# Toeplitz blocks sent through DRAM, and half of the first layer's gate projection in plain float32, in an S5 / HGRN2 / attention trunk

## Chip, cores and metric

The kernel runs on one core of one Trainium2 chip. The metric is the device time of one execution in microseconds (us), as the median of several runs. A core has these engines: PE (TensorE, with PEld for its weight loads), DVE (VectorE), ACT (ScalarE), POOL (GpSimd) and SP (SyncE, which here only issues DMAs).

## What is computed

Four layers on a sequence of 512 tokens of width 1024, each h = h + RMSNorm(branch(RMSNorm(h))). The mixers are S5 (layers 0 and 3), HGRN2 (layer 1) and sliding-window attention (layer 2). The change is in the S5 branch, cut here to what matters:

```python
proj = h @ w_in                      # 1024 -> 2048
u, z = proj[..., :1024], proj[..., 1024:]
xr, xi = B(u)                        # per group of 16 channels: 64 complex states
sr, si = scan(a, xr, xi)             # s_t = a * s_(t-1) + x_t, complex, along the sequence
y = C_re(sr) - C_im(si) + d_skip * u
y = gelu(y)
y = y * sigmoid(y @ w_glu + b_glu)   # the gate projection, 1024 -> 1024
return (y * silu(z)) @ w_out
```

All inputs and the output are float32.

## The kernel before, in words

**Activations** lie with channels on partitions, [128, 8, 512]. A projection runs as 128 x 512 outputs (two of 256 columns for the first four) over eight steps k of 128 channels each. Most matmuls are in float32r with both operands split into a high and a low part (hi, lo), three matmuls a step: hi*hi, hi*lo, lo*hi (`ws_steps`, line 233). Weights are split when they have landed (`w_conv`): ACT copies raw into whi (line 183), DVE subtracts it into wlo (line 184). The input projection of layer 0 is the exception (`plain`, line 156): x stays in one float32 tile xf, the raw weights are used as they are, and a step is one float32 matmul, which the trace shows as two records.

**Weights** come in chunks (256 columns, two pieces of 512 KB; `w_load`, line 153, on SP's queue) in the order of a list: for layer 0 eight chunks of s5_in, four of s5_glu, two of s5_out. Rings of buffers hold them: wraw 3, whi 4, wlo 4. In layer 0 the first piece of each s5_in chunk lies in whi, the second in wraw, and wlo holds parameters (prm) and a table (vt) of the S5 blocks.

**The S5 mixer** works on eight blocks b of eight groups. The sequence is cut into 64 chunks of eight steps. For a block, `s5_v` builds on DVE, from parameters that SP loads (prm), the coefficients q (with a second product q2 of POOL) and the table vt. `s5_taps` takes products of it on PE (kps), copies them to kt (ACT), transposes vt to v (tps) and kt to ktp, and adds the skip term (ksb, line 785); then eight DMAs (line 790) write growing parts of ksb into toep, a Toeplitz block whose zeros were set once. `s5_w` builds w on DVE. `s5_rot` makes the rotation factors. `s5_u` takes the projection out of PSUM, writes it to DRAM (ub, line 819) and reads it back in another layout (u, line 823). `s5_core` multiplies (xps), scans on DVE (line 852), forms the states (spre, line 862), and sums two products, u by toep and states by w (yps, lines 875 and 877), to y, with GELU on ACT and transposes for each pair of blocks (ytp, line 892). In layer 3 the tables were computed ahead, and `s5_load` only loads them.

**The order** of PE, DVE, ACT and SP in an S5 layer is written by a planner (`Flow`). Each piece of work is a generator that yields steps: an engine ("P", "V", "A", "D" for SP's DMAs), an assumed duration, and marks it waits for. The planner always takes the step that can start first, at equal times the one with the lower rank. It counts 0.4 us from one engine to another and 4.5 us behind a DMA. The engines then run in that order. The blocks have ranks 0 to 75, the rest of the input projection (`s5_rest`) 100, the first half of the gate projection (`s5_glu_first`, chunks 0 and 1) 110. A weight load is issued where the code of `s5_rest` or `s5_glu_first` stands, without a step of its own.

One wait is written by hand (line 725): in layer 0 `s5_v` of block b + 1 waits for kt of block b, since kt uses the buffer q12b, in which q2 lies (line 764). In layer 3 kt has its own buffer.

```python
yield "V", 1.3, (m["ap"],) + ((m["kt", b - 1],) if b and j == 0 else ())
```

For the gate projection `s5_yparts` splits y into yh (ACT) and yl (DVE). yl lies in the buffer of x ("xh") and yh in that of its low part ("xl"), so yl can be written only when the input projection is done (mark "rest"). Chunks 2 and 3 of the gate and all of the output projection (`out_proj`, line 248) come after the planned part, in an order that the framework chooses.

**The start** (`run`): x comes in four blocks of 128 tokens, the weights of chunks 0 and 1 between the second and the third. `norm_stats` squares each on ACT (line 279), takes the reciprocal root on POOL (`rstd`) and scales it, in layer 0 on ACT (line 284), in the others on DVE (line 286); `norm_xt` transposes it on PE (line 301), and ACT moves it to xf (line 305).

Of the kernel before, what the change touches and what calls it, by code (L numbers as in the profile page):

```python
# [17 lines left out]
P = 128  # L18
T = 512
# [90 lines left out]
class Trunk:  # L110
# [30 lines left out]
    def w_load(self, i):  # L141
# [17 lines left out]

    def w_conv(self, i):  # L160
# [13 lines left out]
        for raw in raws:  # L174
# [5 lines left out]
            else:  # L180
                hi = self.wpool.tile(shape, F32R, tag="whi", name="whi", bufs=4)
                lo = self.wpool.tile(shape, F32R, tag="wlo", name="wlo", bufs=4)
# [80 lines left out]
    def norm_stats(self, L, tbs, h):  # L263
# [17 lines left out]
        for i, tb in enumerate(tbs):  # L281
            if L == 0:

                nc.scalar.activation(out=xs[:, tb, :], in_=h[:, tb, :], func=AF.Copy, scale=r[:, i:i + 1])
            else:
                self.last_xs = nc.vector.tensor_scalar(out=xs[:, tb, :], in0=h[:, tb, :], scalar1=r[:, i:i + 1], scalar2=None, op0=ALU.mult)
# [336 lines left out]
    def s5_load(self, b, m):  # L623

        nc, s = self.nc, self.scr
        yield "D", 0.2, (m["states", b - 2],) if b > 1 else ()
# [8 lines left out]

    def s5_convs(self, i0, m):

        m["cv", 1].t = 0.0
        for c in range(2, 8):
            yield "A", 2.1, (m["cd", c - 2],) if c > 1 else ()  # L640
            yield "V", 2.6, ()
            self.w_conv(i0 + c)
            self.w_load(i0 + c + 1)
            yield m["cv", c]

    def s5_open(self, j):
# [5 lines left out]
        self.kt = None  # L652
        if j == 0:
            self.s5_params(j)
        else:
            self.s5t = {}
            self.kt = 1
# [6 lines left out]
        self.sp, self.tp, self.cp = [], [], []  # L664
        self.md = s.tile([P, 8, 64], F32, tag="mdec", name="mdec", bufs=1)
        nc.gpsimd.memset(self.md[:, :, 0:1], 0.0)
        for i in range(2):
            t = s.tile([P, 8, 8, 16], F32, tag=f"toep{i}", name="toep", bufs=1)
            nc.gpsimd.memset(t, 0.0)
            self.tp.append(t)  # L670
# [7 lines left out]
    def s5_rot(self, pr, m):  # L678
# [23 lines left out]
        for i in range(2):  # L702

            b = 2 * pr + i
            yield "D", 0.3, (m["states", b - 2],) if pr else ()
# [7 lines left out]
    def s5_v(self, j, b, m):  # L713
# [11 lines left out]
        yield "V", 1.3, (m["ap"],) + ((m["kt", b - 1],) if b and j == 0 else ())  # L725
# [26 lines left out]
    def s5_taps(self, b, m):  # L752
# [11 lines left out]
        kt = self.tab.tile([P, 2, 128], F32, tag="q12b" if self.kt is None else "kt", name="kt", bufs=1)  # L764
# [45 lines left out]
    def s5_u(self, b, ps, m):  # L810
# [6 lines left out]
        yield "D", 0.2, ()  # L817
# [3 lines left out]
        yield "D", 0.2, (m["y", b - 3],) if b > 2 else ()  # L821
# [79 lines left out]
    def s5_rest(self, L, ps, m):  # L901
# [5 lines left out]
        def chunk(c):  # L907
            if plain:
                return self.w_next("s5_in")
# [5 lines left out]
        for half in range(2):  # L915
            c = slice(half * 256, half * 256 + 256)
            for b in range(4):
                if half == 0 and b == 2:
                    if not plain:
                        yield "P", 0.0, (m["cv", 1],)  # L920
# [13 lines left out]
        for c in range(6):  # L934
            if not plain:
                yield "P", 0.0, (m["cv", c + 2],)
# [19 lines left out]
    def s5_yparts(self, pr, yh, yl, free, m):  # L956

        nc, y = self.nc, self.y
        for k in (2 * pr, 2 * pr + 1):
# [4 lines left out]
            yield "V", 0.7, (m["rest"],)  # L964
# [5 lines left out]
    def s5_glu_first(self, glu, y, i0, early, m):  # L970

        w = []
        for c in range(2):
            if early and c == 0:
                yield "A", 2.1, (m["cd", 6],)
                yield "V", 2.6, ()
                self.w_conv(i0 + 8)
                self.w_load(i0 + 9)
                continue
            yield "V", 2.6, (m["rest"],)  # L980
            self.w_conv(self.wi + c)
            self.w_load(self.wi + c + 1)
# [6 lines left out]
        for k in range(KB):  # L989
            for fb in range(4):  # L990
                if k < 6:
                    yield "P", 0.68, (m["yk", k],)
                    if k == 0:
                        steps[fb] = self.ws_steps(glu[fb], w[fb // 2], fb % 2, (y[0][0], y[1][0]), 0, T)
                    next(steps[fb])
        for fb in range(4):
            if fb == 2:
                yield "V", 2.6, ()
                self.w_conv(self.wi)
                self.w_load(self.wi + 1)  # L1000
            for k in (6, 7):
                yield "P", 0.68, (m["yk", k],)
                next(steps[fb])

# [656 lines left out]
```

## Time and profile before

| | us |
|---|---|
| three runs, median (lowest to highest) | 1086.48 (1085.96 to 1090.13) |
| the profiled execution | 1089.59 |
| its span in the trace | 1087.8 |
| S5 of layer 0, from the start to the output projection | 239.4 |
| busy: PE, DVE, ACT, POOL | 1027.0, 746.8, 505.2, 104.4 |

The runs are timed without a profile. The rows come from the profiled execution, whose own time is that of its span and what lies around it. All times in a row are in us from the start of the span unless ns is written.

### The profile page before, as it was taken

The numbers are of one execution on the slowest core, as the hardware profiler recorded it, in microseconds if no ns is written. First come the engines' busy times: TensorE is split into PE (matmuls) and PEld (weight loads), VectorE is DVE, ScalarE is ACT, GpSimd is POOL, SyncE is SP. The second block draws the span as 40 slices with busy tenths as digits, with TensorE's granted clock in tenths as the row PEclk, the third lists the DMA queues.
The fourth block names the chain that finished last, engine by engine and source line by source line (L and its number), as shares of the span: only waits on it lengthen the run. The fifth ranks groups of instructions, "written<-read, shape, count | busy, mean of one in ns | idle before, by whom it ended". The sixth has DMA issues, their size and how long they took to land.

```text
span 1087.8 us, 17048 instructions
## 1 busy us (share of the span) xinstructions
PE 1027.0 (94%) x6480; PEld 816.6 (75%) x6480; DVE 746.8 (69%) x1454; ACT 505.2 (46%) x937; POOL 104.4 (10%) x164
## 2 busy tenths in 40 slices
PE   5999995999999999999999999999999989897997
PEld 3855554777998798998978986666678867676875
DVE  6487789584689778888865664556656687754752
ACT  5234345554552314323244433588844556555531
POOL 2000000030200100000011021100002111000300
PEclk9999997999999999999999999999999999998999
DMA  6375333434432323424253354211223777634221
GB/s 236 79 207 147 96 102 96 157 112 150 149 106 64 126 83 107 156 73 144 67 188 141 97 134 115 59 58 45 79 83 132 212 189 197 205 96 161 96 97 58
DMA packets 70577, 133.31 MB, mean 123 GB/s; under 512 B 28896, under 2 KB 40032, under 8 KB 69472
## 3 DMA queue, kind: packets, MB, share of 16 engines
q1 hardware_dynamic: 65664, 119.04, 35.5%
q10 hardware_dynamic: 4832, 13.19, 3.7%
q8 instruction: 51, 0.84, 0.3%
q14 instruction: 30, 0.25, 0.1%
HBM read 100.51 MB, written 20.15 MB: 111 GB/s over the span
## 4 chain that ended last, share of the span: by engine, by line
PE 66%; DVE 14%; ACT 7%; DMA 5%; issue 5%; POOL 2%; SPq 2%; ACTq 1%; DVEq 0%; POOLq 0%
PE pj L233 27%; PE ops L248 14%; PE zps L248 4%; PE vps L248 3%; PE sps L1138 3%; DVE wlo L184 3%; PE scps L1346 3%; ACT whi L183 2%; PE aops L1382 2%; DMA rsw<-rraw 1%; PE yps L877 1%; SPq L790 1%; PE yps L875 1%; PE ptp L1377 1%; DVE sg L1067 1%
## 5 line engine op out<-in xcount | busy, mean ns | idle before, releaser
L233 PE MATMUL pj<-xh,whi 128*128 128x512 f32 (+1 forms) x496 | 179.9, 364 | 1.2 <-ACT xh L305 0.6
L184 DVE TENSOR_TENSOR wlo<-wraw,whi 128x1024 fp32r<-128x1024 f32 x116 | 144.6, 1262 | 52.4 <-ACT whi L183 45.2
L233 PE MATMUL pj<-xl,whi 128*128 128x512 f32 (+1 forms) x496 | 175.1, 354 | 2.1 <-DVE xl L311 2.1
L233 PE MATMUL pj<-xh,wlo 128*128 128x512 f32 (+1 forms) x496 | 175.4, 354 | 0.0
L183 ACT ACTIVATE whi<-wraw 128x1024 fp32r<-128x1024 f32 x116 | 120.7, 1056 | 73.2 <-PE pj L233 33.5
L233 PE MATMUL pj<-xf,wraw 128*128 128x512 f32 (+1 forms) x320 | 119.6, 524 | 0.4 <-ACT xf L305 0.4
L233 PEld LDWEIGHTS pj<-xh,whi 128*128 128x128 f32 x496 | 93.8, 190 | 17.5 <-issue 5.4
L233 PEld LDWEIGHTS pj<-xl,whi 128*128 128x128 f32 x496 | 94.4, 190 | 13.9 <-DVE xl L311 2.9
L233 PEld LDWEIGHTS pj<-xh,wlo 128*128 128x128 f32 x496 | 94.2, 190 | 13.5 <-issue 1.7
L248 PE MATMUL ops<-whi,gh 128*128 128x512 f32 x256 | 101.7, 398 | 2.7 <-ACT gh L1069 2.1
L248 PE MATMUL ops<-wlo,gh 128*128 128x512 f32 x256 | 100.7, 394 | 1.1 <-DVE wlo L184 1.0
L248 PE MATMUL ops<-whi,gl 128*128 128x512 f32 x256 | 100.5, 395 | 0.0
L233 PEld LDWEIGHTS pj<-xf,wraw 128*128 128x128 f32 x320 | 61.0, 198 | 42.1 <-issue 36.7
L248 PEld LDWEIGHTS ops<-whi,gh 128*128 128x128 f32 x256 | 48.2, 188 | 13.9 <-ACT gh L1069 3.0
L248 PEld LDWEIGHTS ops<-wlo,gh 128*128 128x128 f32 x256 | 48.2, 188 | 13.1 <-DVE wlo L184 2.7
L248 PEld LDWEIGHTS ops<-whi,gl 128*128 128x128 f32 x256 | 48.1, 188 | 11.2 <-DVE gl L1070 0.9
L233 PE MATMUL pj<-yh,whi 128*128 128x512 f32 x128 | 51.1, 399 | 0.0
L233 PE MATMUL pj<-yh,wlo 128*128 128x512 f32 x128 | 50.1, 392 | 0.0
L233 PE MATMUL pj<-yl,whi 128*128 128x512 f32 x128 | 50.1, 392 | 0.0
L354 DVE TENSOR_TENSOR yg<-ops,gpost 128x512 f32<-128x512 f32 x32 | 21.8, 687 | 38.8 <-ACT junk L352 38.8
L248 PE MATMUL vps<-wlo,xh 128*128 128x256 f32 x160 | 45.3, 283 | 0.0
L248 PE MATMUL vps<-whi,xl 128*128 128x256 f32 x160 | 45.3, 283 | 0.0
(279 smaller groups left out, 2100.4 us busy)
## 6 DMA issues: line engine op xcount, KB each, us to landing
wraw<-in_s_in SPq DMA_DIRECT2D x32, 512.0 KB, 4.7
wraw<-in_hg_in SPq DMA_DIRECT2D x32, 512.0 KB, 3.6
wraw<-in_at_in SPq DMA_DIRECT2D x20, 512.0 KB, 4.3
wraw<-in_s_glu SPq DMA_DIRECT2D x16, 512.0 KB, 3.8
wraw<-in_s_out SPq DMA_DIRECT2D x16, 512.0 KB, 3.5
hd<-h SPq DMA_DIRECT2D x6, 1024.0 KB, 4.0
prm<-in_s_bc SPq DMA_DIRECT2D x16, 256.0 KB, 3.8
ub<-ut SPq DMA_DIRECT2D x16, 256.0 KB, 3.7
```

Source lines behind the costliest of these rows:

```text
L183: nc.scalar.activation(out=hi, in_=raw, func=AF.Copy)
L184: nc.vector.tensor_tensor(out=lo, in0=raw, in1=hi.bitcast(F32), op=ALU.subtract)
L233: self.nc.tensor.matmul(ps, lhsT=l[k // 4][:, k % 4, c], rhs=r[:, k, n0:n1], start=k == 0 and n == 0, stop=k == KB - 1 and n == len(terms) ...
L248: self.nc.tensor.matmul(ps, lhsT=l[:, k, c], rhs=r[k // per][:, k % per, :], start=k == 0 and n == 0, stop=k == KB - 1 and n == 2)
L354: nc.vector.tensor_tensor(out=yg[:, tb, f], in0=ps, in1=gp[:, f], op=ALU.mult)
L790: nc.sync.dma_start(out=toep[128 - n:128, jj, :, :], in_=ksb[0:n].rearrange("p a g h -> p (a g) h"))
L875: nc.tensor.matmul(o, lhsT=u[:, g, :], rhs=d["toep"][:, :, g, :], start=True, stop=False)
L877: nc.tensor.matmul(o, lhsT=sp[:, g, :], rhs=d["w"][:, g, :], start=False, stop=True)
L1067: nc.vector.tensor_tensor(out=sg, in0=sg, in1=y[:, k, :], op=ALU.mult)
L1138: nc.tensor.matmul(ps[:, c, :], lhsT=k[:, c * 128:c * 128 + 128], rhs=q4[:, c, :, 1, :], start=True, stop=True)
L1346: nc.tensor.matmul(ps[:, bb, lo:256], lhsT=self.q[r, 4 * p + 2 * b2 + bb, qs], rhs=self.k[r, p, ks], start=True, stop=True)
L1382: nc.tensor.matmul(ops[64 * i:64 * i + 64].rearrange("p b q -> p (b q)"), lhsT=self.v[:, n - 1 + f, kv * 64:kv * 64 + 64], rhs=pts[i][:, f ...
```

## The change

1. `plain` now includes chunks 0 and 1 of layer 0's s5_glu: both are used raw, in float32, against y itself and not against yh and yl. Chunk 0 lies in whi with both pieces, chunk 1 in whi and wraw. Chunk 2 is split into the four wlo buffers, chunk 3 into the four whi buffers. The steps of `s5_glu_first` wait, in layer 0, for y of their pair of blocks, and the planner counts 0.86 us a step.
2. Loads of weights become steps of the plan: `s5_loads` (layer 0, chunks 1 to 10) and "D" steps in `s5_convs` and `s5_glu_first`. The splitting of gate chunk 2 is a line of its own (`s5_glu_conv`). Assumed durations of several DMA steps rise from 0.2 or 0.3 to 0.5 or 1.1.
3. kt lies, in layer 0, in the buffer "pw" (used only while the tables are built), and the wait on line 725 is dropped.
4. ksb is written to a DRAM tile of 240 rows whose first 112 rows are zeros (written once, at the start, by two DMAs on ACT's queue). One DMA then reads the whole Toeplitz block back, partition p and step j from row p + 16 j. This is for both S5 layers; toep is a new tile for each block.
5. At the start all four blocks of x are loaded before chunk 1 of the weights; blocks 0 and 1 are normalised together, and DVE scales them in layer 0 too.

```diff
     def w_load(self, i):
...
-                raw = self.wpool.tile(shape, F32, tag=("whi", "wraw")[v], name="wraw", bufs=(4, 3)[v])
+                t = v if self.wseq[i] != self.GLU0[0] else 0
+                raw = self.wpool.tile(shape, F32, tag=("whi", "wraw")[t], name="wraw", bufs=(4, 3)[t])
...
-        return i < len(self.wseq) and self.wseq[i][:2] == ("s5_in", 0)
+        return i < len(self.wseq) and (self.wseq[i][:2] == ("s5_in", 0) or self.wseq[i] in self.GLU0[:2])
+
+    GLU0 = [("s5_glu", 0, c) for c in range(4)]
...
+                th, tl = "whi", "wlo"
+                if self.wseq[i] in self.GLU0:
+                    th = tl = ("wlo", "whi")[c - 2]
+                hi = self.wpool.tile(shape, F32R, tag=th, name="whi", bufs=4)
+                lo = self.wpool.tile(shape, F32R, tag=tl, name="wlo", bufs=4)
...
-            if L == 0:
-
-                nc.scalar.activation(out=xs[:, tb, :], in_=h[:, tb, :], func=AF.Copy, scale=r[:, i:i + 1])
-            else:
-                self.last_xs = nc.vector.tensor_scalar(...)
+            self.last_xs = nc.vector.tensor_scalar(...)
...
+    def s5_loads(self, i0, m):
+
+        for c in range(1, 11):
+            yield "D", 1.0, (m["cd", min(c - 3, 7)],) if c > 2 else ()
+            self.w_load(i0 + c)
+            yield m["cv", c]
...
+            zero = s.tile([112, 128], F32, tag="t2", name="zero", bufs=1)
+            nc.gpsimd.memset(zero, 0.0)
+            self.kd = []
+            for i in range(2):
+                self.kd.append(self.dram.tile([240, 128], F32, tag=f"kd{i}", name="kd", bufs=1))
+                nc.scalar.dma_start(out=self.kd[i][0:112], in_=zero)
...
-        yield "V", 1.3, (m["ap"],) + ((m["kt", b - 1],) if b and j == 0 else ())
+        yield "V", 1.3, (m["ap"],) + ()
...
-        kt = self.tab.tile([P, 2, 128], F32, tag="q12b" if self.kt is None else "kt", name="kt", bufs=1)
+        kt = self.tab.tile([P, 2, 128], F32, tag=self.kt, name="kt", bufs=1)
...
-        yield "D", 0.6, (m["y", b - 2],) if b > 1 else ()
-        d["toep"] = toep = self.tp[b % 2]
-        for jj in range(8):
-            n = (jj + 1) * 16
-            nc.sync.dma_start(out=toep[128 - n:128, jj, :, :], in_=ksb[0:n].rearrange("p a g h -> p (a g) h"))
+        yield "D", 0.5, (m["toep", b - 2],) if b > 1 else ()
+        kd = self.kd[b % 2]
+        nc.sync.dma_start(out=kd[112:240], in_=ksb.rearrange("p a g h -> p (a g h)"))
+        yield "D", 0.5, (m["y", b - 2],) if b > 1 else ()
+        d["toep"] = toep = self.tab.tile([P, 8, 8, 16], F32, tag=f"toep{b % 2}", name="toep", bufs=1)
+
+        src = bass.AP(tensor=kd.tensor, offset=kd.offset, ap=[[128, P], [16 * 128, 8], [1, 128]])
+        nc.sync.dma_start(out=toep.rearrange("p j g h -> p j (g h)"), in_=src)
...
-            yield "V", 0.7, (m["rest"],)
+            yield "V", 0.7, (m["rest"],) + ((m["w", 7],) if free else ())
...
+        step, free = 0.68, not early
         for c in range(2):
+            if free:
+                step = 0.86
+                yield "P", 0.0, (m["cv", 8 + c],)
+                self.w_conv(i0 + 8 + c)
+                continue
...
-                    yield "P", 0.68, (m["yk", k],)
+                    yield "P", step, (m["yc", k // 2] if free else m["yk", k],)
...
+    def s5_glu_conv(self, i0, free, m):
+
+        if free:
+            yield "V", 2.6, (m["w", 7], m["cv", 10])
+        else:
+            yield "V", 2.6, (m["half"],)
+        self.w_conv(i0 + 10)
+        yield "D", 1.0, ()
+        self.w_load(i0 + 11)
...
                 if tb == 1:
                     self.w_load(0)
-                    self.w_load(1)
-            for tb in range(4):
-                self.norm_stats(self.layers[0], (tb,), x0)
+            for tbs in ((0, 1), (2,), (3,)):
+                self.norm_stats(self.layers[0], tbs, x0)
```

## Rows read from the trace of the kernel before

**Rows 1.** The page: TensorE's busy time, and its granted clock in 40 slices.

```profile
PE 1027.0 (94%) x6480; PEld 816.6 (75%) x6480; DVE 746.8 (69%) x1454; ACT 505.2 (46%) x937; POOL 104.4 (10%) x164
...
PEclk9999997999999999999999999999999999998999
```

**Rows 2.** Busy times by stretch: us, then PE, PEld, DVE, ACT, POOL, clock, DMA.

```profile
20.84:164.73 143.89, 143.15 (x853) 85.75 (x853) 104.53 (x157) 54.16 (x102) 6.98 (x12) 1.00 0.45 121
164.73:217.50 52.77, 39.70 (x325) 31.97 (x325) 38.00 (x47) 29.17 (x42) 3.89 (x4) 0.87 0.41 126
183.20:190.90 7.70, 7.62 (x89) 6.21 (x89) 6.45 (x8) 2.87 (x5) 0.00 (x0) 0.62 0.01 2
217.50:239.36 21.86, 21.86 (x99) 18.08 (x97) 19.56 (x21) 12.54 (x20) 8.67 (x6) 1.00 0.35 110
97.15:156.30 59.15, 58.43 (x377) 31.12 (x376) 47.47 (x60) 23.62 (x41) 3.49 (x6) 1.00 0.37 100
850.00:990.00 140.00, 126.67 (x1116) 101.67 (x1115) 101.06 (x126) 77.83 (x125) 11.19 (x14) 0.96 0.61 177
```

**Rows 3.** Timeline of PE in layer 0: start, us, instruction, idle time before.

```profile
156.05 8.75 PE L233 MATMUL pj<-xf,wraw 128*128 128x512 f32 x20
...
183.20 1.08 PE L762 MATMUL kps<-vt,c 128*32 128x128 f32 x16 [9.11 <-DVE vt L748]
...
207.59 0.60 PE L892 MATMUL ytp<-cst,ysb 128*128 128x128 f32 x4
```

**Rows 4.** Timeline of DVE in layer 0, around one block's ksb.

```profile
136.54 0.29 DVE L785 TENSOR_TENSOR ksb<-ktp,dmx 128x128 f32<-128x128 f32 x1 [6.01 <-PE ktp L779]
136.75 0.74 DVE L730 TENSOR_TENSOR q<-prm,co 128x256 f32<-128x256 f32 x1
...
146.08 0.68 DVE L862 TENSOR_TENSOR spre<-r,rsw 128x504 f32<-128x504 f32 x1
```

**Rows 5.** The start: timeline of ACT and PE, and DVE's scaling in the other layers.

```profile
9.79 2.19 ACT L284 ACTIVATE xs<-x,rs_r 128x1024 f32<-128x1024 f32 x2
...
20.84 11.03 PE L233 MATMUL pj<-xf,wraw 128*128 128x256 f32 x40 [0.40 <-ACT xf L305]
...
L286 DVE TENSOR_SCALAR xs<-h,rs_r x12: 747/753/2619, 270.2 to 841.2; 128x1024 f32<-128x1024 f32 x12
```

**Rows 6.** Timeline of SP in layer 0: the Toeplitz issues of one block.

```profile
136.86 5.00 SPq L790 DMA_DIRECT2D toep<-ksb  x8
```

**Rows 7.** DMA issues: count, KB each, median us to landing.

```profile
wraw<-in_s_glu SPq DMA_DIRECT2D x16, 512.0 KB, 3.8
...
ub<-ut SPq DMA_DIRECT2D x16, 256.0 KB, 3.7
u<-ub SPq DMA_DIRECT2D x16, 256.0 KB, 3.0
...
w<-sd SPq DMA_DIRECT2D x8, 512.0 KB, 4.7
...
toep<-ksb SPq DMA_DIRECT2D x16, 64.0 KB, 1.9
```

**Rows 8.** Groups by line, 0 to 300 us: busy, mean ns, idle before.

```profile
L184 DVE TENSOR_TENSOR wlo<-wraw,whi 128x1024 fp32r<-128x1024 f32 x20 | 24.6, 1252 | 6.8 <-ACT whi L183 6.6
...
L183 ACT ACTIVATE whi<-wraw 128x1024 fp32r<-128x1024 f32 x20 | 20.6, 1053 | 6.3 <-DMA wraw<-in_s_out 2.4 <-DMA wraw<-in_s_glu 1.5 <-PE ops L248 1.2
```

**Rows 9.** Layer 3: waits of PE (us, times, longest), then timelines of SP and DVE.

```profile
PE yps L877 <- DVE spre L862: 5.2, 2, 4.9
PE kps L762 <- DVE vt L748: 3.7, 1, 3.7
PE yps L875 <- DMA toep<-ksb: 3.5, 2, 2.7
...
925.80 5.78 SPq L790 DMA_DIRECT2D toep<-ksb  x8
...
937.51 0.43 DVE L730 TENSOR_TENSOR q<-prm,co 128x256 f32<-128x256 f32 x1 [3.12 <-DMA prm<-in_s_bc]
```

More of the change, by code (lines that the diff above doesn't have):

```diff
@@ L281, in norm_stats @@
         for i, tb in enumerate(tbs):
-            if L == 0:
-                nc.scalar.activation(out=xs[:, tb, :], in_=h[:, tb, :], func=AF.Copy, scale=r[:, i:i + 1])
-            else:
-                self.last_xs = nc.vector.tensor_scalar(out=xs[:, tb, :], in0=h[:, tb, :], scalar1=r[:, i:i + 1], scalar2=None, op0=ALU.mult)
+            self.last_xs = nc.vector.tensor_scalar(out=xs[:, tb, :], in0=h[:, tb, :], scalar1=r[:, i:i + 1], scalar2=None, op0=ALU.mult)
     def norm_xt(self, L, tbs):
@@ L625, in s5_load @@
         nc, s = self.nc, self.scr
-        yield "D", 0.2, (m["states", b - 2],) if b > 1 else ()
+        yield "D", 1.1, (m["states", b - 2],) if b > 1 else ()
         f = self.rot[b] = s.tile([P, 2, 512], F32, tag=f"rot{b % 2}", name="rotf", bufs=1)
@@ L651, in s5_open @@
         self.tab = s = self.tabcm.__enter__()
-        self.kt = None
+        self.kt = ("pw", "kt")[j]
         if j == 0:
@@ L704, in s5_rot @@
             b = 2 * pr + i
-            yield "D", 0.3, (m["states", b - 2],) if pr else ()
+            yield "D", 1.1, (m["states", b - 2],) if pr else ()
             f = s.tile([P, 2, 512], F32, tag=f"rot{i}", name="rotf", bufs=1)
@@ L918, in s5_rest @@
                 if half == 0 and b == 2:
-                    if not plain:
-                        yield "P", 0.0, (m["cv", 1],)
+                    yield "P", 0.0, (m["cv", 1],)
                     w.append(chunk(1))
@@ L934, in s5_rest @@
         for c in range(6):
-            if not plain:
-                yield "P", 0.0, (m["cv", c + 2],)
+            yield "P", 0.0, (m["cv", c + 2],)
             w = chunk(c + 2)
@@ L977, in s5_glu_first @@
                 self.w_conv(i0 + 8)
+                yield "D", 1.0, ()
                 self.w_load(i0 + 9)
@@ L980, in s5_glu_first @@
             yield "V", 2.6, (m["rest"],)
-            self.w_conv(self.wi + c)
-            self.w_load(self.wi + c + 1)
+            self.w_conv(i0 + 8 + c)
+            yield "D", 1.0, ()
+            self.w_load(i0 + 9 + c)
         for c in range(2):
@@ L991, in s5_glu_first @@
                 if k < 6:
-                    yield "P", 0.68, (m["yk", k],)
+                    yield "P", step, (m["yc", k // 2] if free else m["yk", k],)
                     if k == 0:
-                        steps[fb] = self.ws_steps(glu[fb], w[fb // 2], fb % 2, (y[0][0], y[1][0]), 0, T)
+                        steps[fb] = self.ws_steps(glu[fb], w[fb // 2], fb % 2, (self.y, None) if free else (y[0][0], y[1][0]), 0, T)
                     next(steps[fb])
         for fb in range(4):
[L997 to L1000, printed above, removed]
             for k in (6, 7):
-                yield "P", 0.68, (m["yk", k],)
+                yield "P", step, (m["yc", k // 2] if free else m["yk", k],)
                 next(steps[fb])
+            if fb == 1:
+                yield m["half"]
+    def s5_glu_conv(self, i0, free, m):
[4 more added lines that the diff above has]
+        self.w_conv(i0 + 10)
+        yield "D", 1.0, ()
+        self.w_load(i0 + 11)
     def layer_s5(self, L):
```

19 lines of the change are left out of this document (8 added, 11 removed).

## The prediction

> **What bounds the kernel now.** First the page: TensorE is busy 94% of the span, at full clock in nearly every slice [rows 1], so a gain has to come from slices in which it is not. Next, busy times by stretch [rows 2]. In layer 0, from 20.84 to 164.73 us, PE is busy 143.15 of 143.89 us. From 164.73 (the end of the input projection) to 217.50 (the end of the first half of the gate projection, "the half" below) it is busy 39.70 of 52.77 us, and the granted clock is 0.87. From 217.50 to 239.36, which is the second half of the gate projection, it is full again. The reader is to see a dense stage, a hole, a dense stage.
>
> What makes the hole: the longest wait of PE in layer 0 is 9.11 us for vt, of block 7, whose kps starts at 183.20 [rows 3]. The input projection is used up by then, and the gate projection can't fill in: its yl is written into the buffer of x, and its weights are still to be split on ACT and DVE. After the wait PE works at half rate: from 183.20 to 190.90 the clock is 0.62 [rows 2].
>
> Why block 7 is so late: from 97.15 to 156.30 the three blocks are three equal periods of 19.7 us, with DVE busy 47.47 of 59.15 us, 15.8 us a block [rows 2]. In each, DVE stops at ksb until PE has done ktp, 6.01 us in one of them, and the next block's q starts right behind it [rows 4]. That is a loop: q of block b+1 waits for kt of block b (line 725), since kt lies in the buffer of q2. PE meanwhile runs ten steps of the projection (8.75 us, 20 records [rows 3]) before the next kps.
>
> In layer 3 PE is busy 126.67 of 140 us between 850 and 990, clock 0.96 [rows 2]. Its stops are listed in [rows 9]: 5.2, 3.7 and 3.5 us.
>
> **The change part by part.**
>
> *Start of layer 0.* Squares stay on ACT; the scaling leaves it. Today the scalings of blocks 0 and 1 take 2.19 us of ACT together, and those of blocks 2 and 3 are done there too, with PE's operands waiting behind them; PE is dense only from 20.84 [rows 5]. With the change, one rstd serves blocks 0 and 1, DVE scales each in 0.753 us (2.6 at worst [rows 5]), blocks 2 and 3 of x are no longer queued behind chunk 1's weights, and ACT has only squares and evacuations. I put the dense start at about 13 us. What PE does before 20.84 today, eight records of 11.03/40 = 0.276 us and sixteen transposes, is some 4 us at the dense pace and comes after 13 then, so the gain is 20.84 - 13 - 4 = 3.8. On the other side stand four scalings (3.0 us) on a DVE that builds tables then, and two more DMAs on ACT's queue ahead of the constants, which rstd waits for, about 0.45 us each. Bounds: a gain of 6, a loss of 1.
>
> *The loop is cut and the hole is filled.* kt moves to the buffer pw, so q no longer waits. Blocks then go at what DVE needs, 15.8 us, I assume 17, not 19.7; block 7 comes some 20 us earlier, and DVE loses four pieces of weight splitting (1.25 us each; ACT 1.05 each [rows 8]). The first half of the gate projection needs only y and raw weights, so PE has 24 of its 32 steps ready once y of blocks 0 to 5 exists. Price of plain float32: 0.875 us a step (8.75/10 [rows 3]) against 21.86/32 = 0.683 [rows 2]; 32 x 0.192 = 6.1 us more on PE. What is won: 52.77 - 39.70 = 13.1 us of idle time and 0.38 x 7.62 = 2.9 us of half clock, 16.0 together. Fully dense that makes 16.0 - 6.1 = 9.9. I leave a hole of 1.5 and take a gain of 8.4. Bounds: 9.9, and 2 if the last y comes no earlier: its transposes end at 208.2 [rows 3], eight steps of 0.875 behind them at 215.2 at best, and not at 217.5.
>
> *Weights, and the output projection behind.* Loads of chunks 1 to 10 become steps of the plan, due when the buffer is free; landing takes 3.8 us [rows 7], and there are 14 us of PE per chunk (16 x 0.875), so they are covered. Chunk 2 of the gate weights is split in wlo, once block 7's w is done: covered by the first half. Chunk 3's first raw piece waits for the buffer of chunk 1's, free at the end of the half; 3.8 us of landing and 2.3 of splitting stand against 11 us of chunk 2: covered, 5 us to spare. If ACT is late with it, PE waits. Chunk 3 lies in all four whi buffers, so the output projection's weights can be split into them only when chunk 3's matmuls end; the first two pieces can start 2.8 us before. Today two are split ahead. The fourth must also be loaded after the first is split: about 6 us behind that end, needed at 4. I take 1.5 us lost; bounds 0 and 4.
>
> *Toeplitz blocks.* Eight issues a block go (5.00 us of SP [rows 6]); a write of 64 KB to DRAM and a read of 512 KB, in pieces of 512 B, come. The trace has no such pair; nearest are ub (written, 3.7 us) and u (256 KB read back, 3.0) or layer 3's w (512 KB read from DRAM scratch, 4.7) [rows 7]. With two issues of some 0.45 the way from ksb to toep is 3.7 + 3.0 + 0.9 = 7.6 to 3.7 + 4.7 + 0.9 = 9.3 us, against 5.0 + 1.9 = 6.9 now [rows 6, 7]. I take 8.5, nearer to w, which has the same size. A block needs toep when its states are done, at 146.8 where ksb was at 136.5 [rows 4], 10 us later, so the 1.6 us more are covered, with 1.5 us left. What is gained is SP: prm of the next block, today issued behind the eight, goes out earlier. The read waits on SP for the write's landing; behind it stand prm, rotf, u and weights, held up to 3 us where the plan puts nothing between (it allows 4.5).
>
> The Trainium skill, page "DMA: Bandwidth & Descriptors", section "Anatomy of one DMA", has a fixed 2.0 us a transfer plus bytes at 436 GB/s, and says that completion can be surprisingly slow where HBM is the target. By it the pair would be, as an estimate, 2.1 + 3.2 + 0.9 = 6.2 us, shorter than now; the landing of ub here (3.7 us) goes with the warning rather than with the 2.0.
>
> *Layer 3.* Same Toeplitz path, same new costs in the plan; kt had its own buffer already. Lost there: 13.3 us of idle time and 0.04 x 126.7 = 5.1 of half clock. SP's queue stands behind 3.5 us (PE on toep) and 3.7 (PE on vt, after DVE had waited 3.12 for prm, which SP issued behind eight Toeplitz issues of 5.78 us [rows 9]). I take 6: these 7.2 with a part of the clock, less some that the next wait takes (states of block 7, 5.2). Bounds: a gain of 13, a loss of 3, since the order is planned anew.
>
> **Sum:** -3.8 - 8.4 + 1.5 - 6 = -16.7 us. The profiled execution took 1089.59 us (span 1087.8 and 1.8 around it), so 1072.9; it lies 3.1 above the median of the three runs, 1086.48, and against that the forecast is 1069.8 us.
>
> **The rivals.**
> 1. *Only layer 0 gains.* The new plan moves layer 3's stops elsewhere: its longest, 5.2 us for states, is no SP matter. For it: the 6 us is the least certain term. Against: 7.2 us end on SP. -3.8 - 8.4 + 1.5 gives 1075.8. Chance 0.23.
> 2. *The hole stays.* Blocks remain paced by PE's fixed order or by DMAs, and y of block 7 comes as late as now. Then -2 at the start, -2 in the hole, +2 at the output projection, -2 in layer 3: 1082.5. For it: the pace comes from a plan. Against: the loop's only cause in the code is gone. Chance 0.12.
> 3. *Slower: the round trip is late for every block.* Place: yps, first in PE's order behind toep. If write and read take 12 us from ksb and not 8.5, PE stops 2 us in each of 16 blocks, 32 us: 1086.5 + 32 - 16.7 = about 1102. It decides from 10 us on. For it: the 9.3 us of the upper bound, and SP held by the waiting read. Against: the other transfers get an emptier queue. Chance 0.05.
> 4. *More than forecast.* Layer 3's plan closes most of its 18 us: -3.8 - 9.9 - 13 gives 1059.8. Chance 0.1.
> The forecast itself has 0.5.
>
> **How the numbers follow.** 0.5% (5.4 us) is about what a measurement of this kernel can tell from no change. Faster by more than that, under 1081: the forecast, rivals 1 and 4, and a third of 2: 0.87. Within: most of rival 2, 0.08. Slower: rival 3, 0.05. The range 1059.5 to 1082 takes in rivals 1 and 4 and the edge of 2; rival 3 and the rest of 2 are left out.
>
> **What would show it.** PE's first wait-free stretch from about 13 us; PE busy nearly all the time from the end of the input projection to the end of the first half, at clock 1.00, that half ending near 205 and not at 217.5; the blocks at 16 to 17 us; no wait of ksb for ktp ahead of q. The forecast is wrong if PE waits for toep several times, if the gate steps wait for y of blocks 4 to 7, if PE waits for wlo at the output projection by over 4 us, or if layer 3's 850 to 990 still holds 13 us of idle time.

## The result: 1069.16 us, and the profile after

The changed kernel takes 1069.16 us (median, 1067.38 to 1070.39); the kernel before, run beside it, takes 1086.22. The ratio is 0.983, with a 95% interval of 0.9812 to 0.9847. The forecast was 1069.8.

The profiled execution took 1069.92 us, its span is 1068.1. The page answers to [rows 1]: the clock's gap in layer 0 is gone, those of the later layers stand (its slice of 8 in the middle was a 9 before; the last section comes back to it).

```profile
PE 1023.0 (96%) x6448; PEld 805.9 (75%) x6448; DVE 744.3 (70%) x1454; ACT 495.9 (46%) x929; POOL 103.4 (10%) x159
...
PEclk9999999999999999999999998999999999998999
```

Busy times by stretch, columns as in [rows 2]: from the first dense record to the same moment as before, to the end of the half, the second half of the gate, the start of the output projection, and 140 us of layer 3.

```profile
17.06:164.73 147.67, 145.58 (x1001) 89.26 (x1000) 136.23 (x222) 65.34 (x122) 14.62 (x15) 1.00 0.54 150
164.73:201.71 36.98, 36.98 (x148) 18.15 (x147) 16.45 (x22) 16.79 (x24) 3.60 (x3) 1.00 0.42 143
201.71:223.92 22.21, 22.21 (x99) 18.19 (x97) 17.25 (x19) 10.81 (x18) 7.31 (x6) 1.00 0.15 47
223.92:240.00 16.08, 13.48 (x51) 10.39 (x50) 10.04 (x11) 7.06 (x11) 0.00 (x0) 0.89 0.69 237
834.20:974.20 140.00, 129.02 (x1146) 104.54 (x1147) 102.34 (x134) 82.73 (x136) 11.41 (x16) 0.98 0.65 195
```

The hole is closed: PE is busy for 36.98 of 36.98 us at full clock, where it was busy for 39.70 of 52.77. DVE is at 136.23 of 147.67 us in the stage before, so the blocks come nearly as fast as DVE's work allows. The timeline of PE has the landmarks that [rows 3, 5] had before:

```profile
11.28 2.20 PE L303 MATMUL xtp<-cst,xs 128*128 128x128 f32 x8 [11.28 <-DVE xs L288]
...
17.06 9.35 PE L239 MATMUL pj<-xf,wraw 128*128 128x256 f32 x42
...
180.22 0.60 PE L908 MATMUL ytp<-cst,ysb 128*128 128x128 f32 x4
...
180.65 21.62 PE L239 MATMUL pj<-y,wraw 128*128 128x512 f32 x50
...
201.71 0.79 PE L239 MATMUL pj<-yh,whi 128*128 128x512 f32 x1
...
223.92 0.39 PE L254 MATMUL ops<-whi,gh 128*128 128x512 f32 x1
...
231.05 1.04 PE L254 MATMUL ops<-whi,gh 128*128 128x512 f32 x2 [2.47 <-ACT whi L189]
```

Dense from 17.06 instead of 20.84; the last y at 180.8 instead of 208.2; the half ends at 201.71 instead of 217.50, 15.8 us earlier. At 231.05 stands a stop that was not there before: the output projection waits for its split weights. DVE no longer stands for ktp ahead of q, against 6.01 us in [rows 4] (0.24 us at most at the q of four blocks); the first and the last of them, a ksb between, and the busy times from one to the other:

```profile
99.06 0.41 DVE L743 TENSOR_TENSOR q<-prm,co 128x256 f32<-128x256 f32 x1
...
138.47 0.26 DVE L798 TENSOR_TENSOR ksb<-ktp,dmx 128x128 f32<-128x128 f32 x1
...
148.26 0.42 DVE L743 TENSOR_TENSOR q<-prm,co 128x256 f32<-128x256 f32 x1
...
99.06:148.26 49.20, 49.20 (x324) 26.69 (x321) 47.73 (x60) 21.22 (x37) 5.49 (x6) 1.00 0.58 156
```

From 99.06 to 148.26 are three blocks, 16.4 us each (19.7 before), with DVE busy for 47.73 of the 49.20 us and PE for all of them. SP's timeline shows the two issues that replace the eight of [rows 6]:

```profile
138.76 0.33 SPq L801 DMA_DIRECT2D kd<-ksb  x1
139.21 0.37 SPq L736 DMA_DIRECT2D prm<-in_s_bc  x1
140.31 0.37 SPq L806 DMA_DIRECT2D toep<-kd  x1
```

And of the DMA issues (count, KB each, median us to landing) the two that [rows 7] could not show:

```profile
toep<-kd SPq DMA_DIRECT2D x16, 512.0 KB, 4.6
...
kd<-ksb SPq DMA_DIRECT2D x16, 64.0 KB, 1.7
```

In layer 3 the waits of PE (total, times, longest), against [rows 9]: nothing stands behind SP any more, the states of block 7 are where they were, and 3.4 us for v are new.

```profile
PE yps L893 <- DVE spre L878: 5.2, 2, 5.0
PE xps L854 <- ACT v L786: 3.4, 3, 1.6
PE ops L254 <- ACT gh L1101: 1.1, 1, 1.1
```

### The profile page after: what moved, and what is told of

Its sections match the earlier page's. It is cut to its first block, busy times and chain, and to the rows that moved or that the text cites. A ratio compares the mean times of both kernels' runs of the same rounds, so it can differ in the third digit from the quotient of the medians.

```text
span 1068.1 us, 16783 instructions
## 1 busy us (share of the span) xinstructions
PE 1023.0 (96%) x6448; PEld 805.9 (75%) x6448; DVE 744.3 (70%) x1454; ACT 495.9 (46%) x929; POOL 103.4 (10%) x159
## 4 chain that ended last, share of the span: by engine, by line
PE 75%; DVE 12%; ACT 4%; DMA 4%; issue 3%; POOL 1%; ACTq 1%; DVEq 0%; SPq 0%; POOLq 0%
PE pj L239 32%; PE ops L254 15%; PE zps L254 5%; PE vps L254 3%; PE scps L1378 3%; PE sps L1170 3%; PE aops L1414 2%; DVE wlo L190 2%; DMA rsw<-rraw 2%; PE yps L891 2%; PE yps L893 1%; PE xps L854 1%; PE ptp L1409 1%; DVE sg L1099 1%; PE tps L784 1%
## 5 line engine op out<-in xcount | busy, mean ns | idle before, releaser
L190 DVE TENSOR_TENSOR wlo<-wraw,whi 128x1024 fp32r<-128x1024 f32 x112 | 138.6, 1252 | 62.5 <-ACT whi L189 49.1
L189 ACT ACTIVATE whi<-wraw 128x1024 fp32r<-128x1024 f32 x112 | 116.7, 1055 | 82.6 <-PE pj L239 40.7
L239 PEld LDWEIGHTS pj<-xf,wraw 128*128 128x128 f32 x320 | 58.0, 192 | 34.9 <-issue 30.9
L254 PE MATMUL vps<-whi,xh 128*128 128x256 f32 x160 | 45.3, 283 | 0.0
L354 ACT ACTIVATE junk<-ops 128x512 bf16<-128x512 f32 x32 | 19.0, 594 | 50.3 <-PE ops L254 50.2
L254 PE MATMUL zps<-whi,xh 128*128 128x256 f32 x128 | 38.8, 303 | 0.0
```

What stands on the lines that cost most here:

```text
L189: nc.scalar.activation(out=hi, in_=raw, func=AF.Copy)
L190: nc.vector.tensor_tensor(out=lo, in0=raw, in1=hi.bitcast(F32), op=ALU.subtract)
L239: self.nc.tensor.matmul(ps, lhsT=l[k // 4][:, k % 4, c], rhs=r[:, k, n0:n1], start=k == 0 and n == 0, stop=k == KB - 1 and n == len(terms) ...
L254: self.nc.tensor.matmul(ps, lhsT=l[:, k, c], rhs=r[k // per][:, k % per, :], start=k == 0 and n == 0, stop=k == KB - 1 and n == 2)
L354: nc.scalar.activation(out=junk, in_=ps, func=AF.Square, accum_out=ss[tb][:, c:c + 1])
```

## The experiments

To see where an edit acts, each profile is cut at two marks: the issue of layer 1's first small load on ACT's queue (lb_e), which stands for the end of layer 0 with its output projection, and the last store of h for layer 3 (hd). All in us, from the profiled execution; the ratio is that of the timed runs to the kernel before on the same chip.

| run | layer 0 ends | layers 1 and 2 | layer 3 | ratio (95%) |
|---|---|---|---|---|
| before | 291.8 | 547.3 | 248.7 | 1 |
| after | 278.3 | 546.7 | 243.1 | 0.983 (0.9812 to 0.9847) |
| loop back (e1) | 293.3 | 547.7 | 242.8 | 0.9948 (0.993 to 0.9965) |
| gate split (e2) | 289.8 | 546.4 | 242.9 | 0.9922 (0.9892 to 0.9951) |
| gate split, fair (e5) | 278.2 | 546.0 | 242.6 | 0.9841 (0.9827 to 0.9856) |
| eight DMAs at 0.6 (e3) | 286.1 | 547.9 | 245.3 | 0.9925 (0.9897 to 0.9953) |
| eight DMAs at 5.0 (e6) | 276.6 | 546.6 | 258.3 | 0.9961 (0.9947 to 0.9976) |
| old start (e4) | 281.6 | 544.0 | 243.0 | 0.9849 (0.9815 to 0.9884) |
| before, loop cut alone (e7) | 283.0 | 546.7 | 248.1 | 0.9911 (0.9894 to 0.9927) |
| after, output weights in wlo (e8) | 275.6 | 543.9 | 243.9 | 0.9799 (0.9782 to 0.9817) |
| eight DMAs in layer 0 only (e9) | 277.3 | 546.3 | 243.5 | 0.9829 (0.9801 to 0.9856) |
| old costs in layer 3 (e10) | 277.0 | 543.7 | 242.8 | 0.9809 (0.9777 to 0.9841) |
| e9 with e8 (e11) | 276.1 | 545.2 | 243.0 | 0.9821 (0.9794 to 0.9848) |

No edit touches layers 1 and 2, and yet they spread from 543.7 to 547.9. So a difference of some 3 us in one profile's total, or of 0.003 in the ratio, is not an edit's; the columns of layer 0 and layer 3 are read instead. These columns move too, each being one execution. Layer 0 of e10 is the changed kernel's, and ends 1.3 us earlier; layer 3 is the changed kernel's in e1, e2, e4, e5 and e8, and takes from 242.6 to 243.9. So a difference of less than some 1.5 us there says nothing by itself.

### The loop: put back, and cut alone

Theory: the wait of q for kt is what made block 7 late, and without its cut the rest of the change can't fill the hole. Rival: the new pace comes from SP.

```diff
-        yield "V", 1.3, (m["ap"],) + ()
+        yield "V", 1.3, (m["ap"],) + ((m["kt", b - 1],) if b and j == 0 else ())
...
-        self.kt = ("pw", "kt")[j]
+        self.kt = ("q12b", "kt")[j]
```

> The changed kernel with one thing undone: kt lies again in the buffer of q2 in layer 0, and q of a block waits for kt of the one before. Theory (the loop made the hole): the blocks of layer 0 go at 19 to 20 us again and not at some 15.5; y of block 7 is there 18 to 25 us later than the 180.8 us of the changed kernel, the first half of the gate projection ends 7 to 10 us behind 201.7, and the time is 1075 to 1080. Rival (the raw gate projection alone fills the hole, and the pace of the blocks doesn't matter): within 2 us of 1069.

1083.24 against 1089.63. More was lost than expected: layer 0 ends 15.0 us later than in the changed kernel, and 1.5 later than before the change. The timeline of DVE has the old picture, a stop of 6 us and q right behind ksb:

```profile
132.95 0.29 DVE L798 TENSOR_TENSOR ksb<-ktp,dmx 128x128 f32<-128x128 f32 x1 [6.01 <-PE ktp L792]
133.16 0.73 DVE L743 TENSOR_TENSOR q<-prm,co 128x256 f32<-128x256 f32 x1
...
171.70 0.74 DVE L743 TENSOR_TENSOR q<-prm,co 128x256 f32<-128x256 f32 x1
```

From 133.16 to 171.70 are two blocks, 19.3 us each, with SP's eight issues gone: against the rival. The hole has only moved behind the steps that plain float32 could fill; busy times by stretch:

```profile
190.00:200.00 10.00, 4.21 (x44) 2.16 (x42) 8.24 (x12) 4.93 (x7) 0.00 (x0) 0.94 0.68 215
200.00:210.00 10.00, 6.63 (x40) 5.12 (x39) 0.91 (x2) 5.56 (x7) 1.27 (x1) 0.50 0.15 50
```

One stop in it is not the loop's own. For the last block PE waits for the way through DRAM, whose read is issued 3.42 us behind its write, and no other work covers it here:

```profile
199.51 0.69 PE L891 MATMUL yps<-toep,u 128*64 128x128 f32 x4 [5.79 <-DMA toep<-kd]
```

So the 15.0 us are what the loop costs in the changed kernel, this stop with it, and not the price of the loop by itself.

The other half of the question: the kernel before, with these two lines alone changed as the change has them (kt in "pw", no wait).

> The kernel before with one part of the change alone: kt of layer 0 in the buffer pw, q no longer waits for kt. Theory (the loop made the hole, but the split gate projection and SP's eight issues then hold what it frees): blocks at 15.5 to 17 us, half ends 4 to 10 us earlier than 217.5, ratio 0.991 to 0.996. Rival (the parts add up, and the loop alone is worth its share of the whole, 8 us or more): 0.986 to 0.991. Second rival (nothing without the filler): 0.998 to 1.002.

1077.57 against 1087.17: the cut alone wins 8.85 us of layer 0, and nothing in layer 3 beyond the spread. SP still makes its eight issues, and the blocks come at 16.8 us, four from the first q to the last:

```profile
86.30 0.41 DVE L730 TENSOR_TENSOR q<-prm,co 128x256 f32<-128x256 f32 x1
...
153.43 0.42 DVE L730 TENSOR_TENSOR q<-prm,co 128x256 f32<-128x256 f32 x1
```

So the pace was the loop's, and not SP's. The ratio lies on the border of the two expectations; without plain float32, loads as steps, or the way through DRAM, some two thirds of layer 0's 13.5 us are there.

### Plain float32, against the split gate

Theory: plain float32 fills the hole, so without it several us are lost. The first try split the weights and y for the first half as before:

```diff
-        return i < len(self.wseq) and (self.wseq[i][:2] == ("s5_in", 0) or self.wseq[i] in self.GLU0[:2])
+        return i < len(self.wseq) and (self.wseq[i][:2] == ("s5_in", 0) or False)
...
-        step, free = 0.68, not early
+        step, free = 0.68, False
...
```

> The changed kernel with the first half of layer 0's gate projection split into high and low parts again (from yh and yl, chunks 0 and 1 split on ACT and DVE), all else as changed. Theory (PE needs work that is ready as y comes): PE stands idle 6 to 9 us between the end of the input projection and the end of the half, against 6.1 us less matmul time; the half ends 0 to 3 us later, the time is 1069 to 1073. Rival (plain float32 costs its 6.1 us and the faster blocks alone close the hole): 1063 to 1067, faster than the changed kernel. Second rival (the splitting of chunks 0 and 1 on DVE and yl behind it are the limit, as before the change): over 1075.

1080.37, but this says little: the plan issued the first gate weights at 128.44, and their second buffer is only free after chunk 6. SP stood there for 18.48 us:

```profile
128.44 18.48 SPq L154 DMA_DIRECT2D wraw<-in_s_glu  x2
```

PE then waited 9.42 us for a Toeplitz block behind it. That is a fault of the experiment's plan, not the price of the split. So the same kernel again, with the mark that the buffer really needs:

```diff
-            yield "D", 1.0, (m["cd", min(c - 3, 7)],) if c > 2 else ()
+            yield "D", 1.0, (m["cd", 6 if c == 8 else c - 3],) if c > 2 else ()
```

> As the split first half of the gate projection before, but with the load of its chunk 0 planned for when its second buffer is free (one chunk later), so that SP no longer stands on it in front of a Toeplitz read. Theory (PE needs work that is ready as y comes, and the first run's 9.4 us for toep were only its plan): no wait for toep above 2 us; PE idle 6 to 9 us behind the input projection, ratio to the kernel before 0.983 to 0.989, no better than the changed kernel's 0.983. Rival (plain float32 is not needed once the blocks are faster; it costs its 6.1 us): 0.977 to 0.981.

1069.87 against 1087.17: the changed kernel's time without its plain float32, and layer 0 ends at 278.2, where the changed kernel's ends at 278.3 and 277.0 (e10). The stretch that was the hole:

```profile
164.73:201.71 36.98, 30.76 (x168) 22.85 (x167) 17.56 (x20) 16.69 (x23) 2.82 (x2) 0.95 0.48 171
```

6.2 us of it are idle, which plain float32 fills, at the price of its own longer steps (0.865 us against 0.683, times 32: 5.8). It wins 2.1 us up to the output projection (223.92 against 226.03) and gives most or all of them back there: all four whi buffers hold gate chunk 3, and the output weights are split late.

### The output projection

The changed kernel's stop at 231.05 waits for the fourth piece, whose load (issued at 224.41) waits for a raw buffer, which waits for the splits, which wait for whi. The remedy: split the first two output pieces into wlo, which gate chunk 2 has left.

```diff
                 if self.wseq[i] in self.GLU0:
                     th = tl = ("wlo", "whi")[c - 2]
+                elif self.wseq[i] == ("s5_out", 0, 0):
+                    th = tl = ("wlo", "whi")[len(his) // 2]
```

> The changed kernel with one repair: of layer 0's output projection, chunk 0, the first two pieces are split into the four wlo buffers, which are free when gate chunk 2 is done, and the other two into whi. Theory (PE's 2.47 us at the output projection and the half clock behind it come from the fourth piece, whose load waits for the first to be split): no wait of PE for whi there above 0.5 us, no half clock from 230 to 236, 3 to 4.5 us less than the changed kernel, ratio 0.979 to 0.981. Rival (the gate's last gh, from ACT and DVE, is as late): PE waits for gh instead, gain under 1.5 us, ratio 0.982 to 0.984.

1065.67 against 1087.17, the shortest time of the study. ACT splits them at 214.38 and 215.85, the changed kernel its first one at 222.08:

```profile
214.38 1.04 ACT L191 ACTIVATE whi<-wraw 128x1024 fp32r<-128x1024 f32 x1
...
215.85 1.05 ACT L191 ACTIVATE whi<-wraw 128x1024 fp32r<-128x1024 f32 x1
```

Of PE's waits in layer 0 the one for whi is gone, and the longest that is left behind the start is one for gh:

```profile
PE xtp L305 <- DVE xs L290: 11.0, 1, 11.0
PE ops L256 <- ACT gh L1103: 1.1, 1, 1.1
```

Layer 0 ends at 275.6, 2.7 us earlier than in the changed kernel, less than the 3 to 4.5 expected. Of this 1.4 is the stop, 2.47 us for whi against 1.08 for gh. The other 1.3 can't be put down to the remedy: e10 has the changed kernel's layer 0 with the same stop, and the clock behind it is the other one. The stop in e10, then the 4.95 us behind it in the changed kernel and in e10:

```profile
231.30 0.74 PE L254 MATMUL ops<-whi,gh 128*128 128x512 f32 x2 [2.50 <-ACT whi L189]
...
231.05:236.00 4.95, 4.95 (x15) 3.95 (x16) 4.08 (x4) 3.02 (x5) 0.00 (x0) 0.66 0.55 165
...
231.30:236.25 4.95, 4.95 (x22) 4.06 (x23) 4.68 (x5) 3.36 (x6) 0.00 (x0) 1.00 0.57 167
```

At 0.66 some 1.7 us are lost, at 1.00 none, and e10's layer 0 ends at 277.0. So the remedy is worth the 1.4 us of the stop, and takes away a place where the clock can fall. With it plain float32 ends layer 0 2.6 us before the fair split; a split gate with a remedy of its own was not run. The rest of this run's advantage, 2.8 us in layers 1 and 2, is the spread named above.

### Toeplitz blocks

Theory: the way through DRAM is worth nothing in layer 0 and several us in layer 3. First the eight DMAs again, at the 0.6 us that the old plan counted:

```diff
...
-        yield "D", 0.5, (m["toep", b - 2],) if b > 1 else ()
-        kd = self.kd[b % 2]
-        nc.sync.dma_start(out=kd[112:240], in_=ksb.rearrange("p a g h -> p (a g h)"))
-        yield "D", 0.5, (m["y", b - 2],) if b > 1 else ()
...
+        yield "D", 0.6, (m["y", b - 2],) if b > 1 else ()
+        d["toep"] = toep = self.tp[b % 2]
+        for jj in range(8):
+            n = (jj + 1) * 16
+            nc.sync.dma_start(out=toep[128 - n:128, jj, :, :], in_=ksb[0:n].rearrange("p a g h -> p (a g) h"))
...
```

> The changed kernel with the Toeplitz blocks written by eight DMAs again, in both S5 layers, planned at 0.6 us as before. Theory (SP's queue made layer 3's stops): layer 3 is 4 to 7 us longer again and layer 0 up to 2, in all 1074 to 1078. Rival (layer 3 gains by the new plan of DMA steps and weight loads, not by the way of the Toeplitz blocks): within 1.5 us of 1069.

1080.99 against 1089.63. By the ratio the total came at the theory's upper edge (0.9925 of 1086.22 is 1078.1), its place did not: 2.3 us are lost in layer 3, and 7.8 in layer 0. SP's timeline there:

```profile
170.64 5.00 SPq L800 DMA_DIRECT2D toep<-ksb  x8
175.74 6.50 SPq L154 DMA_DIRECT2D wraw<-in_s_glu  x3
```

The gate weights go out behind the eight. ACT, whose order the plan fixed with 0.6 us in mind, stands 5.14 us at their split, with the last GELU (ysb) and table loads behind it:

```profile
179.56 1.06 ACT L189 ACTIVATE whi<-wraw 128x1024 fp32r<-128x1024 f32 x1 [5.14 <-DMA wraw<-in_s_glu]
180.64 1.28 ACT L1091 ACT_TABLE_LOAD   x1
...
184.82 0.60 ACT L893 ACTIVATE ysb<-yps 128x512 f32<-128x512 f32 x1
```

So the question was whether SP's 5 us hurt, or the plan's not knowing of them. The same kernel with 5.0 in place of 0.6:

> The eight Toeplitz DMAs again, but planned at the 5.0 us that they take of SP and not at 0.6. Theory A (the eight cost where the plan does not know them: ACT was sent to split gate weights that SP had not loaded yet, with the last GELU behind it): most of the 10 us comes back, ratio 0.983 to 0.987, layer 0's out projection ends as early as in the changed kernel within 3 us. Theory B (SP's 5 us a block are the cost, whatever the plan knows): ratio 0.990 to 0.994, as with 0.6 planned.

1082.9 against 1087.17, a ratio past both expectations, and both theories at once: layer 0 comes back in full (276.6), layer 3 goes to 258.3, 15.2 us longer than in the changed kernel. There SP also loads rotation factors and w, and the plan, which now counts 5 us a block for the eight, writes another order, in which PE waits for what ACT and DVE do late:

```profile
PE tps L781 <- ACT y L906: 8.6, 3, 4.1
PE xps L848 <- ACT v L783: 3.6, 4, 1.4
PE pj L239 <- DVE yl L975: 3.5, 1, 3.5
```

SP itself is not full there, since it stands 15.7 us for ksb alone. And with 0.6 counted it made the same eight issues a block, and layer 3 was 2.3 us longer, not 15.2. So it is the order that costs here; which step of it does was not tested.

Then the eight DMAs, at 5.0, in layer 0 alone (under the condition that kt lies in "pw"), and the way through DRAM in layer 3:

> The changed kernel with the eight Toeplitz DMAs back in layer 0 alone, the plan counting 5.0 us of SP for them; layer 3 keeps the way through DRAM. Theory (the way through DRAM is worth nothing in layer 0 and only there to spare SP in layer 3; what the run with eight unplanned DMAs lost in layer 0 was the plan's ignorance): layer 0 ends at 276 to 278.5, layer 3 lasts 242.5 to 244, total within 3 us of the changed kernel, ratio to the kernel before 0.979 to 0.986. Rival (layer 0 needs SP free too, and the run with planned DMAs was a lucky profile): layer 0 ends at 282 or later, ratio 0.987 or more. Second rival (layer 3's loss of 15 us came out of what layer 0 left behind): layer 3 stays over 250, ratio over 0.99.

1068.76 against 1087.54, layer 0 at 277.3, layer 3 at 243.5: the theory. In layer 0 the way through DRAM is worth nothing against eight issues that the plan knows; in layer 3 it is worth 2.3 us against eight counted at 0.6, and 15.2 against eight counted at 5.0. With the mended output projection on top:

> The hybrid, and the first two pieces of the output projection's weights split into the wlo buffers. Theory (the two repairs touch different stages, the blocks and the output projection, so they add): layer 0 ends 2 to 3 us earlier than in the hybrid, at 273 to 276, ratio 0.977 to 0.982. Rival (both won the same microseconds, the place where ACT is late at the end of layer 0): layer 0 ends as in the hybrid, within 1 us, ratio equal to the hybrid's.

1067.72, layer 0 at 276.1: 1.2 us better than the hybrid in this stage, so between the two expectations, and no better than e8 alone. The hybrid's stop for whi is 2.57 us and runs on at full clock, as e10's does, and here the stop is 1.08 for gh: the remedy wins what it won against e10 (1.4). The 2 to 3 us expected came from e8's 2.7, which held the changed kernel's slow stretch. The hybrid adds nothing of its own.

### Layer 3: DRAM or the plan's new costs

With the eight DMAs at 0.6, layer 3 took 245.3, with the old kernel's plan 248.7: so the new costs of other DMAs seemed to carry 3.4 of the 5.6 us, the way through DRAM 2.3. To test it, the old costs in layer 3 and the way through DRAM kept:

```diff
-        yield "D", 1.1, (m["states", b - 2],) if b > 1 else ()
+        yield "D", 0.2, (m["states", b - 2],) if b > 1 else ()
...
-            yield m["cv", c]
-            yield "D", 1.0, ()
             self.w_load(i0 + c + 1)
+            yield m["cv", c]
...
-        yield "D", 0.5, ()
+        yield "D", 0.5 if self.kt == "pw" else 0.2, ()
         ub = self.dram.tile([8, 128, 64], F32, tag="ub", name="ub", bufs=8)
...
```

> The changed kernel with layer 3's plan counting as before: 0.2 us for the loads of rotation factors, ub and u, and the loads of weights issued behind the split without a step of their own. Theory (of the 5.6 us that layer 3 gained, 2.3 are the way through DRAM, the other 3.3 the plan's new DMA steps, and the two add): layer 3 lasts 245.5 to 247.5, against 243.1, layer 0 and the rest unchanged, ratio 0.985 to 0.988. Rival (the way through DRAM alone carries it, since SP is then free and the costs no longer matter): layer 3 lasts 242.5 to 244, ratio 0.981 to 0.985.

1066.34 against 1087.54, and layer 3 takes 242.8 us: the rival. The way through DRAM is enough for all of the gain; the new costs help only beside the eight issues (245.3 with them, 248.7 without). Which wait is the longest has changed, its size has not; waits of PE in layer 3:

```profile
PE pj L239 <- DVE yl L980: 5.4, 1, 5.4
PE yps L892 <- DVE spre L877: 1.3, 2, 0.9
```

5.4 us for yl stand where 5.0 for the states of block 7 stood. Both are DVE's work at the end of the blocks, so that is the next place to look in layer 3; no run took it away.

### The start

```diff
                 if tb == 1:
                     self.w_load(0)
+                    self.w_load(1)
-            for tbs in ((0, 1), (2,), (3,)):
-                self.norm_stats(self.layers[0], tbs, x0)
+            for tb in range(4):
+                self.norm_stats(self.layers[0], (tb,), x0)
```

and the scaling of layer 0 back on ACT.

> The changed kernel with the old start: chunk 1 of the weights ahead of the third block of x, each block normalised alone, scaled on ACT. Theory (PE is the bound from the start to the output projection, so what the start gains is kept): 5 to 6 us more, 1074 to 1075.5, the first transposes of block 2 near 31.7 us and not at 26.2. Rival (DVE's tables, which the new start puts off, set when the blocks run, so the start is given back): within 2 us of 1069.

1071.68 against 1089.63. Layer 0 ends 3.3 us later, less than the 5 to 6 expected; the ratio moves by 0.002 only, within its interval, so the size rests on the profile's stage. The edit does not bring the old start back whole: the transposes of the third block of x stand at 29.56, where the kernel before has them at 31.70 and the changed one at 26.24. These 3.3 us are the 3.3 at the end of the layer, so what the start gains is kept.

## Why the prediction was right

The total was right within 1 us, in part by luck: in the two profiles the start and the hole won 15.8 us where the sum had 12.2, and the profiles lie 19.7 apart where the medians lie 17.1. The mechanisms came as described, but two of the reasons were not the ones that the sum gave.

*Start, 3.8 forecast.* From dense start to dense start it is 3.8 (20.84 to 17.06), but the gain is 5.5, near the bound of 6. The 40 records behind 20.84 took 11.03 us, 0.276 each, and the 42 behind 17.06 took 9.35, 0.223 each, though the view gives clock 1.00 for both; the next 16 records before the change took 0.226. The sum took 0.276 for the dense pace. Where the same 48 records are done, at the transposes of the third block of x, before and after stand 5.5 us apart:

```profile
31.70 1.04 PE L301 MATMUL xtp<-cst,xs 128*128 128x128 f32 x8
...
26.24 1.04 PE L303 MATMUL xtp<-cst,xs 128*128 128x128 f32 x8
```

Why the records behind 20.84 are slow was not settled. The old start of e4 has 0.223 there, which is why it gives back 3.3 and not 5.5. "Dense from about 13 us" did not come: the transposes and the first six records lie ahead of 17.06, as 13 plus the 4 us that the sum put behind it.

*Loop and hole, 8.4 forecast.* The half ends 15.8 us earlier, 10.3 after the start's 5.5. Idle time from the dense start to the end of the half fell from 13.8 us (0.74 + 13.07) to 2.1; 2.9 of half clock went; plain float32 costs 5.8, by 0.865 us a step, where 6.1 was said. That makes 8.8, so the terms are sized right. The other 1.5 are outside the sum. Nearly all of it is that the blocks' small matmuls (yps, tps, xps, kps; PE's groups up to 224 us) took 49.1 us in place of 53.4, 4.3 less where the half clock explains at most 2.9; why was not settled. Each block took 16.4 us, 17 was assumed, and in layer 0 PE never waited for toep, and 0.3 us for y.

The reason failed at one point. "Loop is cut and the hole is filled" was one term, and read as if plain float32 were the filling. By the runs the loop cut alone is 8.85 us; with the loop back, and the way through DRAM uncovered by it, nothing of layer 0's gain is left; and the split gate, planned fairly, gives layer 0 the same end as plain float32 within the spread. With y 27 us earlier, ACT and DVE split in time but for 6.2 us of PE, which the shorter steps (5.8) repay.

*Output projection, 1.5 lost.* Of 15.8 us at the end of the half, 15.4 are left when the output projection starts and 13.5 at the end of layer 0: 2.3 lost, by the chain that was described (whi full, fourth piece loaded after a split), and by the half clock behind its stop, which the sum left out. In e10, with the same stop and no half clock, some 1 us is lost. This loss takes most or all of what plain float32 gained, and the two lines of e8 recover it.

*Toeplitz, layer 0, counted 0.* Right by e9, and the way was covered; with the loop back it was not, and PE stood 5.79 us for it. From ksb (138.47) to the issue of the read (140.31) are 1.84 us, and its median landing is 4.6: some 6.4 us, where 8.5 was taken and 7.6 was the lower bound. The write of 64 KB lands in 1.7; ub (3.7), of four times the size, was the wrong row for it, and the old toep (1.9), of the same size, the right one. The estimate by the figures of the Trainium skill (page "DMA: Bandwidth & Descriptors", section "Anatomy of one DMA — SWDGE (gpsimd) path"), 6.2 us for the pair, was the nearer one, though the section gives them for DMAs that GpSimd issues, and these go on SP's queue. Its warning about HBM as a target does not show in kd's median of 1.7 us. In layer 3 SP did stand up to 4.1 us for kd's landing, 8.2 in all. Rival 3, which needed 10 us for every block, did not come: PE's waits in layers 0 and 3 have none for toep.

*Layer 3, 6 forecast.* 5.6 measured. That its stops behind SP's queue would go and the 5.2 for the states stay came true to the wait: 5.0 is there, toep and vt are not. That "the order is planned anew" could cost was right as well: e6 shows 15.2 us of it.

Sum of the two profiles: 13.5 + 0.6 + 5.6 = 19.7 us of span, against 17.1 between the medians. Layers 1 and 2 can move by 4 us between executions, so the profiles can't be held against the medians more closely.

## What to carry to other kernels

Where a stage's blocks come at a period longer than the work of any engine in them, look for a buffer that closes a loop through two engines; cutting it was worth more in layer 0 than everything built around it. A planner's assumed DMA cost is part of the kernel, and the true cost need not give the better order: eight issues cost 5.0 us of SP, and counting 0.6 lost 7.8 us in layer 0 and 2.3 in layer 3, while counting 5.0 lost nothing in layer 0 and 15.2 in layer 3. Work that fills a hole must be followed to the ring of buffers behind it, since there it can give back most of what it won.

## What the runs showed of the hardware

**A stop of the same length costs differently.** In layer 2, which no edit touches, PE stops once for q. In the changed kernel the timeline has

```profile
651.92 1.23 PE L1378 MATMUL scps<-k,q 64*128 64x128 f32 x8 [3.58 <-DVE q L1356]
```

and the stretch behind it runs at 1.2 GHz, half clock:

```profile
652.00:658.00 6.00, 6.00 (x22) 4.09 (x22) 4.34 (x17) 1.55 (x3) 0.00 (x0) 0.50 0.54 131
```

In the run with old costs in layer 3 the stop is 2.53 us,

```profile
649.98 0.72 PE L1375 MATMUL scps<-k,q 64*128 64x128 f32 x8 [2.53 <-DVE q L1353]
```

and the clock stays at 2.4 GHz:

```profile
650.70:656.70 6.00, 5.93 (x26) 3.40 (x25) 4.66 (x23) 2.92 (x12) 0.00 (x0) 1.00 0.70 174
```

It is not the length alone that decides. Over the 8 us behind this stop the granted clock was 0.79 in e8, whose stop was 1.91 us, 1.00 in e6 after 2.82, and 0.59 in e9 after 2.63. The stop at layer 0's output projection shows the same for the same code: 0.66 behind 2.47 us in the changed kernel, 1.00 behind 2.50 in e10. So the same stop costs from nothing to some 3 us, which is a part of the spread of layers 1 and 2. The Trainium skill (page "TensorE: Matmul & The Clock Gate", "Part 1: The HAM clock gate") says of the first matmuls of a kernel that how many run slow differs from run to run; these rows show the like for a stop inside a kernel.

**A small write to DRAM lands early as a rule.** kd's 64 KB land in a median of 1.7 us, in DRAM, as fast as the old toep's 64 KB in on-chip memory (1.9 [rows 7]); in the block shown the read that waits for it is issued 1.55 us behind it. It is not always so: in layer 3 SP stood up to 4.1 us for that landing.
